# Sample's small products on 128 rows, head norms in place, and two weights split ahead, in a one-core encoder step

## The chip, the cores and the metric

The kernel runs on one core of one Trainium2 chip, as one launch. The metric is the time of an execution on the device in microseconds. A core has a matrix engine (PE), a vector engine (DVE), an activation engine (ACT), a general engine (POOL) and SP, which issues transfers; POOL issues transfers too. Each engine works through its own queue in order, and waits on semaphores for the others.

## The reference

One layer of a hybrid encoder, for a prompt of 512 tokens and a sample of 64 tokens, both 1024 wide, in fp32:

```python
x = x + mixer(rmsnorm(x))        # gated delta rule (4 heads of 128) and gated linear attention, merged by gates
x = x + cross_attn(rmsnorm(x))   # 4 heads of 256 into 256 memory tokens
x = x + conv_ffn(rmsnorm(x))     # 1024 -> 2*2816, causal conv of width 3, silu gate, -> 1024
y = rmsnorm(x)
```

In the delta rule each chunk needs the inverse of a lower triangular matrix:

```python
a_kk = where(strict, einsum('nbhcd,nbhsd->nbhcs', kb, kc) * decay, 0.0)
wu = triangular_solve(eye + a_kk, rhs, lower=True, unit_diagonal=True)
```

The outputs are both y, and the states of both branches, of the convolutions, and the memory's keys and values. What the text calls Prompt and Sample are the 512 and the 64 tokens.

## The kernel before

Activations stand transposed, features on the 128 partitions and all 576 tokens along the free axis, in 128-feature tiles x. A product with a 1024-wide weight runs over eight such tiles. To keep fp32 accuracy each operand is split into a rounded part and a rest (xh and xl, the weight's two tiles w), and three products are summed: high by high, high by rest, rest by high.

A weight comes twice from HBM. SP loads it to a raw tile (wr). ACT writes its negative to the rest's tile and its rounded copy to the high tile, and POOL issues a DMA that adds the weight once more to the rest's tile (`split_summed`), which leaves the rounding error. So a weight's high part is ready when ACT is through, its rest only when that DMA has landed. Raw tiles are four, weight tiles six until the middle of the kernel. `emit_weight(i)` writes these steps for the i-th weight; `fetch(i)` does so for as many as there are tiles for; `weight(...)` takes a weight and gives the tiles of older ones back.

At the start three weights (the first head's q, k, v) are split part by part while x comes in (`wpart`). PE multiplies all three together (`first3`), 144 matmuls. Then come the copies of its results out of PSUM (`conv_raw`, tiles u, two on DVE and the third on ACT), the squares for the norm (`sq_act`, sums in acc), a small product with w0 on 32 columns, the norm's sums (`ssq`), and the fourth weight (`za`, head 0), which is the second that the wording of the change counts. The norm's factors (rt, by a power on POOL) are spread over the partitions with a diagonal matrix (dg) and ones on PE, give rbc, and scale the gates' rows (ba).

All other work is written as chains (generators): `c_gdn(h)` for a delta-rule head, h = 0 to 3 for Prompt and 4 for all heads of Sample; `c_gla(p)` for a pair of linear-attention heads; `c_att(hd)` for an attention head. A planner (`Driver`) runs them beside the main sequence of projections. It keeps a clock for PE and lists of busy times for DVE, ACT and POOL, with costs per instruction and due times of tiles, and it writes each engine's instructions in order of planned start, up to 6 us (BACK) ahead of PE's place. The order on each engine is fixed thereby when the kernel is built. When a buffer comes free is part of the plan, so the number of slots (NS, of SLOT columns each) has a say in the order. X stands for DVE or POOL, whichever the plan finds earlier.

Line 292 of the profile is the recording helper's one call, and stands for all planned instructions; so groups are told apart by the tiles' names. sm is any PSUM bank.

In `c_gdn` the inverse is built in five levels (LEVELS 2, 4, 8, 16, 32). A level transposes the odd blocks of the inverse so far (xo, in xi) on PE, multiplies the odd keys (no, from N) with its even blocks, masks that (bd), multiplies with the transposed copy (yc), and subtracts. For Prompt n = 128 rows, two of each product a level; for Sample n = 64, one of each. An fp32 matmul that is no transpose is recorded as two passes. For Prompt a lower block is then made with N and T2 (tile T): rows 0 to 63 cleared by POOL, rows 64 to 127 copied by DVE.

`head_norm` and `head_norms` take the squares of the outputs ot (or os), scale into a new slot (on) and transpose that. In `c_att` probabilities e stand in three tiles, two for Prompt and one with 64 rows for Sample, and are transposed on PE.

Of the kernel before, what the change touches and what calls it, by code (L numbers as in the profile page):

```python
# [17 lines left out]
P = 128  # L18
D = 1024
TP = 512  # L20
# [2 lines left out]
KT = D // P  # L23
EPS = 1e-6
NJ = 22
SLOT = 584
HT = T // 2
NS = 57
RAWB = 4
NBANK = 8  # L30
SPARE = 2
# [481 lines left out]
def tile_trunk(ctx, tc, xT, memT, wt, wd, vec, cst, w0, wgate, st_gdn, st_conv, st_gla, st_ffn, ckT, cv,  # L513
# [344 lines left out]

    def sum_tile(w=T):
        acc = slot("acc")  # L860
        G.memset(acc[:, w:w + 8], 0.0)
        return acc

    def ssq(accs, t, n, ps):
# [8 lines left out]
    def c_rstat(key, accs, n, sample, delay, out=None, at=TP):  # L873

        yield [accs[0][0]]
        rt = cp.tile([P, 8], F32, name=nm("rt"))
        ps = sm()
        for t in range(n):
            ssq(accs, t, 128, ps)
        rin = tiny(8, "rin")  # L880
        k = n
        if sample:
            k += 1
            ssq(accs, n, 72, ps)
            G.memset(rin, 1.0)
            V.tensor_scalar(rin[0:64, n:n + 1], ps[0:64, n:n + 1], 1.0 / D, EPS, op0=ALU.mult, op1=ALU.add)
        V.tensor_scalar(rin[:, 0:n], ps[:, 0:n], 1.0 / D, EPS, op0=ALU.mult, op1=ALU.add)
        G.tensor_tensor(rt[:, 0:k], rin[:, 0:k], mhalf[:, 0:k], op=ALU.pow)
        yield
        rh, rl = cp.tile([P, 8], F32R, name=nm("rh")), cp.tile([P, 8], F32, name=nm("rl"))  # L890
        V.tensor_copy(rh[:, 0:k], rt[:, 0:k])
        V.tensor_tensor(rl[:, 0:k], rt[:, 0:k], f(rh[:, 0:k]), op=ALU.subtract)
        dgs = []
        for r_ in (f(rh), rl):
            dg = slot("dg", F32R)
            V.tensor_tensor(r4(dg[:, :n * 128]), ident.unsqueeze(1).broadcast_to([P, n, 128]),
                            r_[:, 0:n].unsqueeze(2).broadcast_to([P, n, 128]), op=ALU.mult)
            if sample:
                V.tensor_scalar(dg[:, TP:TP + TS], ident[:, 0:64], r_[:, n:n + 1], None, op0=ALU.mult)
            dgs.append(dg)  # L900
        yield
        out = out or slot("rbc")
        ps = sm()
        for i, dg in enumerate(dgs):
            PE.matmul(ps[:, :n * 128], ones_r, dg[:, :n * 128], start=i == 0, stop=i == 1)
        A.copy(out[:, :n * 128], ps[:, :n * 128])
        if sample:
            ps2 = sm()
            for i, dg in enumerate(dgs):
# [173 lines left out]
    def head_norms(*tiles):  # L1083
# [10 lines left out]
        yield  # L1094
        ons = []
        for (o3, n, k), ss in zip(tiles, sums):
            on3 = r4(slot("on")[0:n, 0:128 * k])
            V.tensor_tensor(on3, o3, ss[0:n, 0:k].unsqueeze(2).broadcast_to([n, k, 128]), op=ALU.mult)
            ons.append(on3)
        yield  # L1100
# [8 lines left out]
    def head_norm(o3, n, k, box, rq=None):  # L1109
# [13 lines left out]
        on = slot("on")  # L1123
        on3 = r4(on[0:n, 0:128 * k])
# [10 lines left out]
    def c_gdn(h):  # L1135
# [91 lines left out]
        V.tensor_tensor(col(SX), col(SX), pd[0:n, 0:4], op=ALU.mult)  # L1227

        xi = slot("xi")
        for i in range(4):  # L1230
            V.scalar_tensor_tensor(xi[0:n, n * i:n * i + n], pk[0:n, n * i:n * i + n], rr[0:n, 4 * SX + i:4 * SX + i + 1],
                                   negm1[0:n, 0:n], op0=ALU.mult, op1=ALU.mult)
# [8 lines left out]
            return ap.rearrange("p (a s b) -> p a s b", s=2, b=b)[:, :, 0, :]  # L1241

        def odd_keys(li):
            no = small(f"no{me}", 2, 256)
            A.copy(no[0:n, 0:w].rearrange("p (a b) -> p a b", b=LEVELS[li]), odd(N_.rearrange("p a b -> p (a b)"), LEVELS[li]))
            return no

        no = odd_keys(0)
        xo = small(f"xo{me}", 1, 256)
# [10 lines left out]
        for li, b in enumerate(LEVELS):  # L1260
            pt = sm()
            for c in range(w // 128):
                PE.transpose(pt[:, n * c:n * c + n], xo[0:n, 128 * c:128 * c + 128], ident[0:n, 0:n])
            yc = small(f"yc{me}", 1, 256)
            if n == 128:
                A.copy(yc[:, 0:256], pt[:, 0:256])
# [1 line left out]
                A.copy(r4(yc[:, 0:128], 64), pt[:, 0:64].unsqueeze(1).broadcast_to([P, 2, 64]))  # L1268
            p1 = sm()
            for c in range(w // 128):  # L1270
                PE.matmul(p1[:, 128 * c:128 * c + 128], no[0:n, 128 * c:128 * c + 128], even(xi[0:n, 256 * c:256 * c + 256], b), start=True, stop=True)
            bd = small(f"bd{me}", 1, 256)
            lm = const(M_LEV + 128 * li)
            V.tensor_tensor(r4(bd[:, 0:w]), r4(p1[:, 0:w]), lm.unsqueeze(1).broadcast_to([P, w // 128, 128]), op=ALU.mult)
            if b < LEVELS[-1]:
                no = odd_keys(li + 1)
                xo = small(f"xo{me}", 1, 256)
# [21 lines left out]
        A.copy(yt[0:n, 0:W], px[0:n, 0:W])  # L1299
        if n == 128:  # L1300
            pt2 = sm()
            tt = slot("T2")
            G.memset(tt[0:64, 0:256], 0.0)
            for i in range(4):
                PE.matmul(pt2[64:128, 64 * i:64 * i + 64], N_[:, i, 64:128], xi3[:, i, 0:64], start=True, stop=True)
            V.tensor_copy(tt[64:128, 0:256], pt2[64:128, 0:256])
            yield
            pu = sm()
# [39 lines left out]
        for i in range(4 if h < 4 else 0):  # L1348
            ci = 4 * i + h
            if S is not None:  # L1350
                pc = sm()
                PE.matmul(pc[0:n, 0:128], ks_[i], S, start=True, stop=True)
                R = small("R", 4)[0:n, :]
# [41 lines left out]
    def c_gla(p):  # L1395
# [35 lines left out]
            yield WAIT  # L1431
        ks = N["kb", p]
        kx, kg = slot("kx"), slot("kg")
        G.memset(kg[:, T:T + 8], 0.0)
# [7 lines left out]
        PE.transpose(pt2[0:72, 0:128], kg[:, TP:T + 8], ident)  # L1442
# [103 lines left out]
    def c_att(hd):  # L1546
# [4 lines left out]
        for g in range(3):  # L1551
# [14 lines left out]
            V.tensor_reduce(sc[0:n, 0:cnt_], r4(pss[0:n, 0:256 * cnt_], 256), axis=AX.X, op=ALU.max)  # L1566
            V.tensor_scalar(sc[0:n, 0:cnt_], sc[0:n, 0:cnt_], -1.0 / 16, None, op0=ALU.mult)
            e = slot("e")
            for i in range(cnt_):
                A.activation(e[0:n, 256 * i:256 * i + 256], pss[0:n, 256 * i:256 * i + 256], AF.Exp,  # L1570
                             bias=sc[0:n, i:i + 1], scale=1.0 / 16, accum_out=sc[0:n, 2 + i:3 + i])
# [21 lines left out]
        A.copy(pst, pS[:, 0:128])  # L1593
        yield
        while not drv.ready(("v", hd)):
            yield WAIT
# [114 lines left out]
    def main():  # L1711
# [895 lines left out]
```

## Time and profile before

| | |
|---|---|
| median of 3 runs | 1081.94 us (1079.63, 1081.94, 1083.07) |
| profiled execution | 1078.61 us, span from first to last instruction 1076.8 us |
| mean granted clock of PE | 0.997 |
| busy: PE, DVE, ACT, POOL | 99%, 70%, 66%, 34% |
| moved | 171 MB, a mean of 159 GB/s |

A row of the time line reads: start and length in us, engine, line, operation, tile written <- tiles read, rows and columns of the array (PE), shape, count of merged instructions, and in brackets the idle time ahead and what ended it. PE's records overlap, since matmuls are pipelined: what one costs is seen from start to start.

### The profile page before, as it was taken

How to read it: one execution, taken by the hardware profiler on the slowest of the kernel's cores; microseconds unless marked ns; L12 is line 12 of the kernel's file. 1: busy time of each engine (PE TensorE's matmuls, PEld its weight loads, DVE VectorE, ACT ScalarE, POOL GpSimd, SP SyncE). 2: the span in 40 equal slices, each digit the busy share in tenths (PEclk: the TensorE clock that was granted, in tenths of full speed). 3: DMA queues.
4: the chain of work that ended last, by engine and by line, in shares of the span. 5: the costliest groups of instructions: out<-in, count | busy, mean ns of one | idle time of the engine just before them, and what ended most of it. 6: DMA issues, size and time to landing. Idle time of an engine off the chain costs nothing.

```text
span 1076.8 us, 21403 instructions
## 1 busy us (share of the span) xinstructions
PE 1065.5 (99%) x8162; PEld 1048.5 (97%) x8162; DVE 751.3 (70%) x1472; ACT 706.9 (66%) x1410; POOL 363.4 (34%) x584
## 2 busy tenths in 40 slices
PE   9899999999999999999999999999999999999997
PEld 8899999999999999999999999999999999999997
DVE  6666854767665776878647766778877776678665
ACT  6665546564667577456666678768776775777645
POOL 0334225344434333114211235344343333332324
PEclk9999999999999999999999999999999999999999
DMA  7656354454437979679674368758887798778844
GB/s 270 158 124 154 61 135 110 95 123 106 99 58 167 252 171 199 237 208 238 172 186 138 63 161 198 180 115 166 185 192 173 153 217 189 181 159 190 185 87 109
DMA packets 68182, 171.33 MB, mean 159 GB/s; under 512 B 7920, under 2 KB 14576, under 8 KB 68080
## 3 DMA queue, kind: packets, MB, share of 16 engines
q0 software_dynamic: 30672, 71.19, 38.4%
q1 hardware_dynamic: 36976, 98.26, 27.6%
q8 instruction: 64, 1.05, 0.4%
q10 hardware_dynamic: 432, 0.53, 0.1%
q14 instruction: 38, 0.31, 0.1%
HBM read 157.50 MB, written 5.37 MB: 151 GB/s over the span
## 4 chain that ended last, share of the span: by engine, by line
PE 95%; DMA 2%; ACT 1%; DVE 1%; issue 0%; POOL 0%; ACTq 0%; DVEq 0%; POOLq 0%
PE sm L292 95%; DMA w<-wt 2%; ACT w L292 1%; PE warm L292 0%; DVE on L292 0%; ACT jk L292 0%; DVE ws L292 0%; DVE x L292 0%; DVE gt L292 0%; DVE acl L292 0%; DVE yo L292 0%; ACT ao L292 0%; DVE S L292 0%; ACT ach L292 0%; ACT xh L292 0%
## 5 line engine op out<-in xcount | busy, mean ns | idle before, releaser
L292 PE MATMUL sm<-xh,w 128*128 128x290 f32 (+3 forms) x2304 | 448.6, 301 | 3.7 <-DMA w<-wt 3.2
L292 PEld LDWEIGHTS sm<-xh,w 128*128 128x128 f32 x2304 | 358.8, 190 | 6.2 <-DMA w<-wt 3.7
L292 PE MATMUL sm<-xl,w 128*128 128x290 f32 (+3 forms) x1152 | 270.6, 296 | 0.0
L292 POOL DMA_DIRECT2D w<-wt x152 | 135.1, 898 | 348.3 <-ACT w L292 296.5
L292 PE MATMUL sm<-ach,w 128*128 128x288 f32 (+2 forms) x1212 | 231.4, 296 | 0.2 <-DVE x L292 0.2
L292 PEld LDWEIGHTS sm<-xl,w 128*128 128x128 f32 x1152 | 200.7, 189 | 0.2 <-DVE xl L292 0.2
L292 PEld LDWEIGHTS sm<-ach,w 128*128 128x128 f32 x1212 | 189.8, 188 | 1.2 <-ACT w L292 0.6
L292 ACT CAST w<-wr 128x512 fp32r<-128x512 f32 (+5 forms) x209 | 159.2, 764 | 15.2 <-PE sm L292 9.6
L292 ACT ACTIVATE w<-wr 128x512 fp32r<-128x512 f32 (+5 forms) x186 | 142.2, 765 | 27.0 <-PE sm L292 25.8
L292 PE MATMUL sm<-acl,w 128*128 128x256 f32 (+2 forms) x606 | 146.6, 295 | 0.2 <-DVE acl L292 0.2
L292 ACT CAST w<-ws 128x512 fp32r<-128x512 f32 (+1 forms) x136 | 80.2, 597 | 49.9 <-DVE ws L292 26.9
L292 PEld LDWEIGHTS sm<-acl,w 128*128 128x128 f32 x606 | 107.3, 188 | 0.5 <-DVE acl L292 0.5
L292 DVE TENSOR_TENSOR w<-ws,w 128x512 fp32r<-128x512 f32 (+1 forms) x107 | 72.8, 689 | 22.6 <-ACT w L292 20.8
L292 DVE SCALAR_TENSOR_TENSOR fc<-fu,vec,fc 128x578 f32<-128x578 f32 x88 | 70.5, 816 | 3.3 <-ACT fc L292 3.3
L292 PE MATMUL sm<-sh,w 128*128 128x290 f32 x288 | 61.5, 298 | 0.0
L292 DVE TENSOR_TENSOR x<-x,sm 128x320 f32<-128x320 f32 (+3 forms) x98 | 40.1, 438 | 22.8 <-PE sm L292 22.5
L292 POOL DMA_DIRECT2D w<-wd x34 | 29.8, 886 | 75.1 <-ACT w L292 67.6
L292 ACT ACTIVATE fc<-fu,vec 128x578 f32<-128x578 f32 x44 | 38.1, 871 | 15.1 <-POOL fu L292 14.8
L292 PEld LDWEIGHTS sm<-sh,w 128*128 128x128 f32 x288 | 47.6, 189 | 0.0
L292 PE MATMUL sm<-oh,w 128*128 128x256 f32 (+1 forms) x256 | 44.8, 295 | 0.0
L292 DVE TENSOR_TENSOR ws<-ws,wr 128x512 f32<-128x512 f32 (+1 forms) x66 | 43.8, 663 | 1.0
L292 PE MATMUL sm<-sl,w 128*128 128x290 f32 x144 | 39.7, 297 | 0.0
(391 smaller groups left out, 1947.9 us busy)
## 6 DMA issues: line engine op xcount, KB each, us to landing
wr<-wt SPq DMA_DIRECT2D x129, 512.0 KB, 5.6
w<-wt POOLq DMA_DIRECT2D x51, 512.0 KB, 6.7
w<-wt POOLq DMA_DIRECT2D x101, 256.0 KB, 6.1
w<-ws POOLq DMA_DIRECT2D x27, 256.0 KB, 5.1
x<-xT SPq DMA_DIRECT2D x16, 288.0 KB, 5.9
wr<-wt SPq DMA_DIRECT2D x14, 256.0 KB, 5.2
wr<-wd SPq DMA_DIRECT2D x8, 448.0 KB, 5.0
w<-wd POOLq DMA_DIRECT2D x8, 448.0 KB, 6.7
```

The lines of the kernel that those rows point to most:

```text
L292: fn(*args, **kw)
```

## The change

- Sample's inverse: xi takes a whole slot on 128 rows, of which POOL clears rows 64 to 127; xo and no are columns 256 to 511 of the same slot. The transposes and the first product of each level use all 128 rows. In attention rows 64 to 127 of Sample's e are cleared, and its two transposes use 128 rows. The rows added hold zeros.
- Head norms write the scaled outputs over ot and os.
- T2 lies in N, so that its clear comes after the four products that read N.
- NS goes from 57 to 59, SLOT from 584 to 582, so that the clears and products of the padding have 70 columns instead of 72; R has two buffers instead of four.
- At the start, the four late squares, the giving back of the first three weights, and the emission of weights 3 and 4 are written ahead of the copies of the first product.

```diff
-SLOT = 584
+SLOT = 582
-NS = 57
+NS = 59
...
-            on3 = r4(slot("on")[0:n, 0:128 * k])
+            on3 = o3
             V.tensor_tensor(on3, o3, ss[0:n, 0:k].unsqueeze(2).broadcast_to([n, k, 128]), op=ALU.mult)
...
         xi = slot("xi")
+        rows = P if n == 64 else n
+        if n == 64:
+            G.memset(xi[64:128, 0:512], 0.0)
...
-            no = small(f"no{me}", 2, 256)
+            no = small(f"no{me}", 2, 256) if n == 128 else xi[:, 384:512]
...
-                PE.transpose(pt[:, n * c:n * c + n], xo[0:n, 128 * c:128 * c + 128], ident[0:n, 0:n])
+                PE.transpose(pt[:, 128 * c:128 * c + 128], xo[0:rows, 128 * c:128 * c + 128], ident)
...
-                PE.matmul(p1[:, 128 * c:128 * c + 128], no[0:n, 128 * c:128 * c + 128], even(xi[0:n, 256 * c:256 * c + 256], b), start=True, stop=True)
+                PE.matmul(p1[:, 128 * c:128 * c + 128], no[0:rows, 128 * c:128 * c + 128], even(xi[0:rows, 256 * c:256 * c + 256], b), start=True, stop=True)
...
-            tt = slot("T2")
-            G.memset(tt[0:64, 0:256], 0.0)
             for i in range(4):
                 PE.matmul(pt2[64:128, 64 * i:64 * i + 64], N_[:, i, 64:128], xi3[:, i, 0:64], start=True, stop=True)
+            tt = N_[:, 0:2, :].rearrange("p a b -> p (a b)")
+            G.memset(tt[0:64, 0:256], 0.0)
...
+            if g == 2:
+                G.memset(e[64:128, 0:256], 0.0)
...
-            PE.transpose(pS[:, 64 * mt_:64 * mt_ + 64], probs[2][0:64, 128 * mt_:128 * mt_ + 128], ident[0:64, 0:64])
+            PE.transpose(pS[:, 128 * mt_:128 * mt_ + 128], probs[2][:, 128 * mt_:128 * mt_ + 128], ident)
...
+        for k in range(4, KT):
+            sq_act(k)
+        for i in range(3):
+            drop(*wready.pop(i))
+        emit_weight(3)
+        emit_weight(4)
         raw_u = [conv_raw(ps, copy) for ps, copy in zip(first3, (V.tensor_copy, V.tensor_copy, A.copy))]
         fetch(3)
-        for k in range(4, KT):
-            sq_act(k)
```

How the order moves, at three places. On ACT, at the start, behind the squares (sq); wr is a raw weight, w a split one, u a copy of the first product. Before:

```order
L292 ACTIVATE sq_317<-x_89 128x576
L292 COPY u_313<-sm_135 128x256
L292 COPY u_313<-sm_136 128x256
L292 COPY u_313<-sm_136 128x64
L292 ACTIVATE w_357<-wr_355 128x1024
L292 CAST w_356<-wr_355 128x1024
L292 ACTIVATE w_360<-wr_358 128x1024
L292 CAST w_359<-wr_358 128x1024
```

and now:

```order
L292 ACTIVATE sq_314<-x_89 128x576
L292 ACTIVATE w_317<-wr_315 128x1024
L292 CAST w_316<-wr_315 128x1024
L292 ACTIVATE w_320<-wr_318 128x1024
L292 CAST w_319<-wr_318 128x1024
L292 COPY u_323<-sm_135 128x256
L292 COPY u_323<-sm_136 128x256
L292 COPY u_323<-sm_136 128x64
```

The four instructions of both splits moved ahead of the three copies.

On POOL, at the same place; the DMA rows are the adding transfers, rt the norm's power. Before:

```order
L292 MEMSET rin_353 128x8
L292 DMA w_357<-wt 128x1024
L292 ISA
L292 TENSOR_TENSOR rt_341<-rin_353,mhalf 128x5
L292 DMA w_360<-wt 128x1024
L292 DMA w_363<-wt 128x1024
```

and now:

```order
L292 DMA w_317<-wt 128x1024
L292 MEMSET rin_366 128x8
L292 DMA w_320<-wt 128x1024
L292 MEMSET u_321 128x3
L292 DMA w_326<-wt 128x1024
L292 ISA
L292 TENSOR_TENSOR rt_353<-rin_366,mhalf 128x5
```

Three transfers, not one, now stand ahead of the power.

On PE, at the second delta-rule head, where T2 (now in N) is used; R and vg belong to the first head's chain, xh are projections. Before:

```order
L292 MATMUL sm_2067<-xi_1589,N_1586 64x64 x4
L292 MATMUL sm_2075<-R_2051,Y_1677 128x128
L292 MATMUL sm_1953<-xh_124,w_1643 128x256
L292 MATMUL sm_1954<-xh_124,w_1643 128x320
L292 MATMUL sm_1953<-xh_126,w_1643 128x256
L292 MATMUL sm_1954<-xh_126,w_1643 128x320
L292 MATMUL sm_2087<-Y_2066,T_2068 64x64 x4
```

and now:

```order
L292 MATMUL sm_2066<-xi_1589,N_1586 64x64 x4
L292 MATMUL sm_2072<-R_2050,Y_1677 128x128
L292 MATMUL sm_1952<-xh_124,w_1643 128x256
L292 MATMUL sm_1953<-xh_124,w_1643 128x320
L292 MATMUL sm_1952<-xh_126,w_1643 128x256
L292 MATMUL sm_1953<-xh_126,w_1643 128x320
L292 MATMUL sm_2089<-xh_112,w_1819 128x256
L292 MATMUL sm_2090<-xh_112,w_1819 128x320
L292 MATMUL sm_2089<-xl_113,w_1819 128x256
L292 MATMUL sm_2090<-xl_113,w_1819 128x320
L292 MATMUL sm_2096<-Y_2065,N_1586 64x64 x4
```

Four matmuls of the next projection moved ahead of the use.

More of the change, by code (lines that the diff above doesn't have):

```diff
@@ L860, in sum_tile @@
         acc = slot("acc")
-        G.memset(acc[:, w:w + 8], 0.0)
+        G.memset(acc[:, w:w + 6], 0.0)
         return acc
@@ L883, in c_rstat @@
             k += 1
-            ssq(accs, n, 72, ps)
+            ssq(accs, n, 70, ps)
             G.memset(rin, 1.0)
@@ L1122, in head_norm @@
         yield
-        on = slot("on")
-        on3 = r4(on[0:n, 0:128 * k])
+        on3 = o3
         V.tensor_tensor(on3, o3, ss[0:n, 0:k].unsqueeze(2).broadcast_to([n, k, 128]), op=ALU.mult)
@@ L1248, in c_gdn @@
         no = odd_keys(0)
-        xo = small(f"xo{me}", 1, 256)
+        xo = small(f"xo{me}", 1, 256) if n == 128 else xi[:, 256:384]
         A.copy(xo[0:n, 0:w].rearrange("p (a b) -> p a b", b=2), odd(xi[0:n, 0:W], 2))
@@ L1276, in c_gdn @@
                 no = odd_keys(li + 1)
-                xo = small(f"xo{me}", 1, 256)
+                xo = small(f"xo{me}", 1, 256) if n == 128 else xi[:, 256:384]
                 xo_ = xo[0:n, 0:w].rearrange("p (a s b) -> p a s b", s=2, b=b)
@@ L1352, in c_gdn @@
                 PE.matmul(pc[0:n, 0:128], ks_[i], S, start=True, stop=True)
-                R = small("R", 4)[0:n, :]
+                R = small("R", 2)[0:n, :]
                 V.scalar_tensor_tensor(R, pc[0:n, 0:128], sg[0:n, NE, ci:ci + 1], vb[:, i, :], op0=ALU.mult, op1=ALU.add)
@@ L1433, in c_gla @@
         kx, kg = slot("kx"), slot("kg")
-        G.memset(kg[:, T:T + 8], 0.0)
+        G.memset(kg[:, T:T + 6], 0.0)
         V.tensor_tensor(kg[:, 0:T], ks[:, 0:T], e3[:, 0:T], op=ALU.mult)
@@ L1441, in c_gla @@
         pt2 = sm()
-        PE.transpose(pt2[0:72, 0:128], kg[:, TP:T + 8], ident)
+        PE.transpose(pt2[0:70, 0:128], kg[:, TP:T + 6], ident)
         for a in range(2):
@@ L1590, in c_att @@
         for mt_ in range(2):
-            PE.transpose(pS[:, 64 * mt_:64 * mt_ + 64], probs[2][0:64, 128 * mt_:128 * mt_ + 128], ident[0:64, 0:64])
+            PE.transpose(pS[:, 128 * mt_:128 * mt_ + 128], probs[2][:, 128 * mt_:128 * mt_ + 128], ident)
         pst = small("pst", 2)
-        A.copy(pst, pS[:, 0:128])
+        A.copy(r4(pst, 64), r4(pS[:, 0:256])[:, :, 0:64])
         yield
```

## The prediction

> **What bounds the kernel now.** I read the page first, then PE's waits, the chain in order of time, and the time lines of the stages that the change touches.
>
> ```profile
> PE 1065.5 (99%) x8162; PEld 1048.5 (97%) x8162; DVE 751.3 (70%) x1472; ACT 706.9 (66%) x1410; POOL 363.4 (34%) x584
> PE sm L292 <- DMA w<-wt: 3.2, 2, 2.8
> PE sm L292 <- ACT gt L292: 0.4, 1, 0.4
> PE sm L292 <- DVE T L292: 0.2, 1, 0.2
> ```
>
> PE is busy for 99% of the span. It waits for one thing of any size, a weight DMA. So a microsecond saved on DVE, ACT or POOL is worth nothing, and one saved on PE, as a wait or as a slot of the array, counts in full unless a later wait takes it back.
>
> **The start: the second weight.** PE's time line (start, length) round that wait, ACT's and POOL's beside it, two pieces of the chain, and two windows (the number after the engines is the granted clock, then the DMA share):
>
> ```profile
> 32.37 0.42 PE L292 MATMUL sm<-xh,w 128*128 128x256 f32 x2
> 32.63 0.43 PE L292 MATMUL sm<-xl,w 128*128 128x256 f32 x2
> 35.90 0.80 PE L292 MATMUL sm<-xh,w 128*128 128x256 f32 x4 [2.84 <-DMA w<-wt]
> 36.54 0.77 PE L292 MATMUL sm<-dg,onesr 128*128 128x512 f32 x4
> 37.15 3.18 PE L292 MATMUL sm<-xh,w 128*128 128x256 f32 x12
> 40.12 1.41 PE L292 MATMUL sm<-cst,ba 128*128 128x8 f32 x10
> 15.62 4.12 ACT L292 ACTIVATE sq<-x 128x576 f32<-128x576 f32 x7
> 25.43 0.77 ACT L292 COPY u<-sm 128x256 f32<-128x256 f32 x3 [5.69 <-PE sm L292]
> 26.07 1.08 ACT L292 ACTIVATE w<-wr 128x1024 fp32r<-128x1024 f32 x1
> 27.46 1.05 POOL L292 DMA_DIRECT2D w<-wt  x1 [24.57 <-ACT w L292]
> 29.20 1.19 POOL L292 TENSOR_TENSOR rt<-rin,mhalf 128x5 f32<-128x5 f32 x1 [0.69 <-DVE rin L292]
> 6.06 19.34 PE sm L292 x143
> 27.46 8.39 DMA w<-wt
> 22.00:25.40 3.40, 3.40 (x27) 3.30 (x25) 1.54 (x6) 0.00 (x0) 0.00 (x0) 1.00 0.02 6
> 37.14:40.56 3.42, 3.42 (x18) 3.42 (x17) 2.30 (x6) 1.17 (x4) 1.10 (x4) 0.51 1.08 279
> ```
>
> ACT stands idle for 5.69 us behind the copies of the first product, which need PE's end at 25.43. Only after them comes the split of the second weight (26.07), then the adding DMA, issued at 27.46 and landed 8.39 later, at 35.85. PE had run out at 32.63 + 0.26 = 32.89 (rows stand 0.26 apart), so it lost 35.90 - 32.89 = 3.0 us.
>
> The change puts both splits before the copies. ACT is free at 15.62 + 4.12 = 19.74. The raw weight has landed by 22.00 at the latest, since the DMA share is 0.02 from there on. So the split starts between 19.7 and 22.0, POOL issues 1.4 later as now (27.46 - 26.07), at 21.1 to 23.4, and with 8.39 to land the sum is there at 29.5 to 31.8. That is 1.1 to 3.4 us before PE asks. The tiles it writes are those of the first two weights, which PE last reads at one and two thirds of the product that runs from 6.06 to 25.40, so at 12.5 and 19.0: free in time. SP's next raw loads wait for these splits and move ahead with them, into a stretch with a DMA share of 0.02. The wait goes: **3.0 us**. Bounds 3.0, and 0 if the earlier issue finds something that the trace can't show; both ends of the computed landing give 3.0, and I take it.
>
> The second loss stands right behind. In the window 37.14:40.56 the granted clock was 0.51. Twelve matmuls took 40.12 - 37.15 = 2.97; at the spacing before the gap they take 6 x 0.26 = 1.56, with 0.09 for the first after the fp32 ones (0.22 against 0.13 in the rows further down) 1.65. So 1.3 us more goes if PE is not left idle. Bounds 0 and 1.3, and I take **1.3**, since the slow window begins right behind that gap. [...]
>
> What is late next? PE reaches the normalizer's diagonal (dg) and the gates' operand (ba) 3.0 us earlier, and ba with 1.3 us less ahead of it.
>
> ```profile
> 32.08 1.12 DVE L292 TENSOR_SCALAR dg<-keep,rl 128x64 fp32r<-128x64 f32 x1
> 37.82 0.82 DVE L292 TENSOR_TENSOR ba<-sm,rbc 128x256 f32<-128x256 f32 x2 [4.62 <-ACT rbc L292]
> ```
>
> dg is complete at 33.20. PE comes to dg at 36.54 - 3.0 = 33.5, and first to its wide half. ba is complete 1.49 after 37.15; PE needs it 1.65 after. Both just fit, by 0.3 and 0.16 us. POOL's power (rt, 29.20) now stands behind three DMA issues instead of one. The third follows the third split, which moves up to about 26.1 on ACT, so it ends near 27.46 + 1.05 = 28.5, before rin frees rt at 29.2. Cost 0; if that cover goes, rt, dg and PE slip together.
>
> **The products on 64 rows.** One level of Sample's inverse in PE's time line, 64-row rows first, then 128-row fp32 ones, and the same for attention with the count of forms:
>
> ```profile
> 313.62 0.29 PE L292 MATMUL sm<-xl,w 128*128 128x288 f32 x1
> 313.85 0.27 PE L292 MATMUL sm<-keep,xo 64*128 64x64 f32 x1
> 313.95 0.44 PE L292 MATMUL sm<-xi,no 64*128 64x128 f32 x2
> 314.32 0.40 PE L292 MATMUL sm<-xh,w 128*128 128x288 f32 x1
> 314.56 0.29 PE L292 MATMUL sm<-xl,w 128*128 128x288 f32 x1
> 314.69 0.39 PE L292 MATMUL sm<-R,Y 128*128 128x128 f32 x2
> 314.83 0.38 PE L292 MATMUL sm<-xh,w 128*128 128x288 f32 x1
> 315.05 0.29 PE L292 MATMUL sm<-xl,w 128*128 128x288 f32 x1
> 328.40 0.60 PE L292 MATMUL sm<-keep,on 128*128 128x128 f32 x4
> 328.75 0.77 PE L292 MATMUL sm<-xh,w 128*128 128x288 f32 x4
> 556.50 1.30 PE L292 MATMUL sm<-keep,e 128*128 128x128 f32 x10
> 557.74 0.53 PE L292 MATMUL sm<-xh,w 128*128 128x256 f32 x2
> L292 PE MATMUL sm<-keep,xo x45: 270/272/328, 87.7 to 329.5; 128*128 128x128 f32 x40, 64*128 64x64 f32 x5
> L292 PE MATMUL sm<-keep,e x40: 222/272/275, 556.5 to 618.7; 128*128 128x128 f32 x32, 64*128 64x64 f32 x8
> ```
>
> Starts tell what a matmul costs the array. Two fp32 passes on 128 rows take 314.83 - 314.69 = 0.14, four take 0.35, so one more is 0.105. The first ordinary one behind takes 0.22 (314.83 to 315.05) instead of 0.13. A level's xl, transpose, two passes and xh take 314.56 - 313.62 = 0.94 on 64 rows; on 128 rows 0.13 + (0.14 + 0.105) + 0.22 = 0.60. Saved 0.34, five levels (xo x5): **1.7 us**. Attention's ten transposes, two of them on 64 rows, take 557.74 - 556.50 = 1.24; ten on 128 rows 0.35 + 6 x 0.105 = 0.98. Saved 0.26, four heads (x8 of two): **1.0 us**. Bounds: nothing, if the cost came from elsewhere than the rows, and 2.8, if the slower ordinary matmul behind (0.24) gains its 0.02 too.
>
> [...]
>
> **What is added.** Nine POOL clears: five new ones (Sample's tile, and attention's four heads), and Prompt's four of T2, which ran early and now, in N, wait for the products that read N.
>
> ```profile
> 158.12 0.65 POOL L292 MEMSET T<- 64x256 f32 x1
> 159.48 1.56 POOL L292 MEMSET aqb<- 128x512 f32 x3
> 168.35 0.43 DVE L292 COPY T<-sm 64x256 f32<-64x256 f32 x1 [1.64 <-PE sm L292]
> 169.19 0.68 PE L292 MATMUL sm<-Y,T 128*64 128x64 f32 x8
> 170.65 0.88 POOL L292 DMA_DIRECT2D w<-wt  x1 [9.60 <-ACT w L292]
> ```
>
> At the second head POOL stands idle from 161.0 to 170.6, while DVE copies the other half from 168.35 to 168.78. A clear let go by the same products runs beside that copy (0.65 us at most), and PE, which used T at 169.19, now has four more matmuls (4 x 0.13) ahead of that. Cost 0, by that cover. If it is gone at all nine, 9 x 0.65 = 5.9 us is the upper bound; the lower is 0. Norms in place, the two buffers more, and 70 columns for 72 remove no instruction of weight. They only move the planner's order: PE's order is the old one up to 169 us and again from about 635 us. Between, the waits for gt and T in the first fence (0.6) may go or come again: bounds -0.6 and +2, taken 0.
>
> **The sum**: 3.0 + 1.3 + 1.7 + 1.0 = 7.0 us. The profiled execution took 1078.61 (span 1076.8), 3.3 below the median 1081.94; its like would be 1071.6, and the median 1081.94 - 7.0 = **1074.9**. About 0.3% (3.2 us) is what a measurement tells from no change.
>
> **Rivals.**
> *The clock term is this run's alone* (windows fall otherwise, or a short wait at dg or ba takes its place): for it, 0.16 and 0.3 us of spare are thin; against, 0.51 is plain. 1076.2, still faster. 0.11. [...]
> *The 64-row forms cost no more than the 128-row ones*: against it, every level's rows. 1077.6. 0.02. [...]
> *New waits in the reordered stretch, or behind the clears, take 4 to 7 us*: for it, PE waits for only 0.6 there now, so that another order can hardly take away and can add, and nine clears hang on an in-order queue; against, DVE and ACT have 30% to spare. 1079 to 1082: no change. 0.13.
> *Slower: a clear stands behind a POOL issue that waits for ACT.* The row at 170.65 shows the queue held 9.60 us by one. If PE comes to the use 1.4 after the products let go (169.19 + 0.52 - 168.35), it stands 8.2, and a slow clock window adds 1.3: two such places give 1074.9 + 19 = 1093.9. One gives 1084.4, which is still within 0.3%. It decides from a total wait of 10.2 us on. Against: the order has such an issue right ahead at few of them. 0.05.
> *The waits for gt and T vanish too*: 1074.3, or lower by what other order brings. 0.05.
> My forecast: 0.64. So faster 0.82, same 0.13, slower 0.05. The range runs from 1071.0 (the profiled execution, 1078.61, as base, and the waits for gt and T gone) to 1080.3 (the slowest of the three runs, 1083.07, as base, the clock term and half of the clears' bound lost).
>
> **What would show it.** After: PE's wait for DMA w<-wt at the start gone, POOL's first issue near 21 to 23 us, clock 1.00 between 34 and 42; no 64-row keep,xo, keep,e; levels at 0.60 us. Wrong if PE waits for POOL (N, e, xi, rt), if dg or ba become its releaser, or if the middle shows new waits for ACT or DVE of over 3 us.

## The result, and the profile after

The changed kernel takes 1069.79 us (median of 5 runs, 1069.41 to 1070.45). The kernel before took 1081.94 in 5 runs beside it (1079.16 to 1083.63). The ratio is 0.9896, interval 0.9877 to 0.9916: 12.15 us faster. The forecast of 1074.9 had the direction, but 1069.8 lies below its range, which began at 1071.0. Run beside the kernel before once more (experiment 5), the change gave 0.9911 (0.9898 to 0.9925), 9.44 us.

The profiled executions took 1078.61 and 1069.41 us, 9.20 apart. Span and busy times on the page of the changed kernel:

```profile
span 1067.6 us, 21403 instructions
PE 1059.3 (99%) x8162; PEld 1044.6 (98%) x8162; DVE 749.7 (70%) x1480; ACT 705.0 (66%) x1410; POOL 356.5 (33%) x581
```

Two of the largest waits of PE for products that are left (us in total, times, longest):

```profile
PE sm L292 <- ACT gt L292: 0.4, 1, 0.4
PE sm L292 <- DMA w<-wt: 0.3, 1, 0.3
```

The wait for weights was 3.2 in two places and is 0.3 in one: at the start PE no longer waits for one, and the 0.3 stands between 619 and 719 us, where the kernel before had 0.4. PE is still busy for 99%, with 6 us less to do: half-clock time and slow 64-row products are counted as busy (in the first trace of before 3.41 of 3.41 us from 37.21 on, at a clock of 0.50, and 0.94 of 0.94 us in the level from 313.62 to 314.56), so the share could not show them.

At the start, the time lines of PE, ACT, POOL and DVE in the changed kernel:

```profile
32.31 0.43 PE L292 MATMUL sm<-xl,w 128*128 128x256 f32 x2
32.58 0.69 PE L292 MATMUL sm<-xh,w 128*128 128x256 f32 x4
33.11 0.77 PE L292 MATMUL sm<-dg,onesr 128*128 128x512 f32 x4
33.71 1.84 PE L292 MATMUL sm<-xh,w 128*128 128x256 f32 x12
35.40 1.17 PE L292 MATMUL sm<-cst,ba 128*128 128x8 f32 x10
16.10 4.12 ACT L292 ACTIVATE sq<-x 128x576 f32<-128x576 f32 x7
20.16 1.06 ACT L292 ACTIVATE w<-wr 128x1024 fp32r<-128x1024 f32 x1
25.10 0.77 ACT L292 COPY u<-sm 128x256 f32<-128x256 f32 x3 [1.05 <-PE sm L292]
21.53 1.05 POOL L292 DMA_DIRECT2D w<-wt  x1 [18.68 <-ACT w L292]
27.11 0.86 POOL L292 DMA_DIRECT2D w<-wt  x1 [2.71 <-ACT w L292]
28.88 1.20 POOL L292 TENSOR_TENSOR rt<-rin,mhalf 128x5 f32<-128x5 f32 x1 [0.90 <-DVE rin L292]
34.39 0.82 DVE L292 TENSOR_TENSOR ba<-sm,rbc 128x256 f32<-128x256 f32 x2 [2.37 <-ACT rbc L292]
```

And its window where the granted clock had been 0.51 (the clock is the third number from the end):

```profile
37.14:40.56 3.42, 3.42 (x22) 2.70 (x21) 3.00 (x9) 2.59 (x6) 0.93 (x1) 1.00 0.01 4
```

The rest part's first product (32.58) now follows the high part's last (32.31) without a gap. The split starts at 20.16, right behind the squares, and the adding DMA is issued at 21.53. Twelve matmuls that took 2.97 from start to start take 1.69 (33.71 to 35.40), at a clock of 1.00.

One level of Sample's inverse, and one head's ten transposes, in PE's time line of the changed kernel:

```profile
321.89 0.30 PE L292 MATMUL sm<-acl,w 128*128 128x288 f32 x1
322.03 0.27 PE L292 MATMUL sm<-keep,xi 128*128 128x128 f32 x1
322.13 0.39 PE L292 MATMUL sm<-xi 128*128 128x128 f32 x2
322.28 0.38 PE L292 MATMUL sm<-ach,w 128*128 128x288 f32 x1
322.49 0.29 PE L292 MATMUL sm<-acl,w 128*128 128x288 f32 x1
550.83 1.25 PE L292 MATMUL sm<-keep,e 128*128 128x128 f32 x10
551.84 1.42 PE L292 MATMUL sm<-xh,w 128*128 128x256 f32 x9
```

From product to product the level takes 322.49 - 321.89 = 0.60 (it was 0.94), the ten transposes 551.84 - 550.83 = 1.01 (it was 1.24).

**Where the 9.1 us of the traces lie.** Both kernels issue 8162 matmuls, so each can be set against the one of the same number. By how much the changed kernel is ahead, at times of the kernel before:

| at | ahead, us | gained since the row above |
|---|---|---|
| 13 us | 0.32 | 0.32, warm-up |
| 60 us | 4.97 | 4.65, the start |
| 304 us | 5.61 | 0.64, reordered stretch |
| 332 us | 7.42 | 1.81, Sample's inverse |
| 440 us | 6.49 | -0.93 |
| 556 us | 6.73 | 0.24 |
| 619 us | 7.85 | 1.12, four attention heads |
| end | 9.09 | 1.24 |

The two kernels issue their matmuls in different orders round 304 us, so that row is rough. What stands in it and in the next is sure only in sum, 2.45: from product to product the five levels of Sample's inverse take 2.94 instead of 4.67, and the waits for gt (0.4, between 320 and 330 us) and T (0.2, between 260 and 290) are gone. The warm-up is no gain: two more executions of the unchanged kernel differ from the first there by 0.26 and 0.39. The loss before 440 us is for the most part one new wait, seen in the time lines of ACT and PE of the changed kernel:

```profile
403.59 1.06 ACT L292 ACTIVATE w<-wr 128x1024 fp32r<-128x1024 f32 x1 [0.63 <-ACT gt L292]
404.56 1.03 ACT L292 CAST w<-wr 128x1024 fp32r<-128x1024 f32 x1
405.49 1.25 ACT L292 ACTIVATE gt<-gt 128x576 f32<-128x576 f32 x2
406.00 0.70 PE L292 MATMUL sm<-xh,w 128*128 128x288 f32 x4
407.08 0.40 PE L292 MATMUL sm<-ach,w 128*128 128x288 f32 x1 [0.38 <-ACT gt L292]
```

The plan puts a 2 us weight split ahead of the gates (gt), and PE comes to a stop for their bank: four matmuls take 1.08 from start to start instead of 0.53.

### The profile page after: what moved, and what is told of

The parts are those of the page before. It is cut to its first block, busy times and chain, and to the rows that moved or that the text cites. A ratio compares the mean times of both kernels' runs of the same rounds, so it can differ in the third digit from the quotient of the medians.

```text
span 1067.6 us, 21403 instructions
## 1 busy us (share of the span) xinstructions
PE 1059.3 (99%) x8162; PEld 1044.6 (98%) x8162; DVE 749.7 (70%) x1480; ACT 705.0 (66%) x1410; POOL 356.5 (33%) x581
## 4 chain that ended last, share of the span: by engine, by line
PE 96%; DMA 1%; ACT 1%; issue 0%; DVE 0%; SPq 0%; ACTq 0%
PE sm L292 96%; DMA w<-wt 1%; ACT w L292 1%; DMA wr<-wt 0%; ACT gt L292 0%; DVE w L292 0%; DVE x L292 0%; DVE acl L292 0%; DVE yo L292 0%; ACT ao L292 0%; ACT ach L292 0%; ACT xh L292 0%; DVE xl L292 0%; SPq L292 0%; DVE ws L292 0%
```

## The experiments

The kernel before ran beside each series: medians 1078.61 (23 runs, with experiments 1 to 4), 1078.82 (15, with 5 to 8), 1078.33 (9, with 9 to 12) and 1078.76 (23, with 13 and 14). "Below" and "above" are against the one of its series; the interval follows.

**1. The start alone** (edit to the kernel before)

```diff
+        for k in range(4, KT):
+            sq_act(k)
+        for i in range(3):
+            drop(*wready.pop(i))
+        emit_weight(3)
+        emit_weight(4)
         raw_u = [conv_raw(ps, copy) for ps, copy in zip(first3, (V.tensor_copy, V.tensor_copy, A.copy))]
         fetch(3)
-        for k in range(4, KT):
-            sq_act(k)
```

> The kernel before with one part of the change: late squares, giving back of the first three weights, and weights 3 and 4 ahead of the copies of the first product. Theory A (the forecast's two terms, wait 3.0 and clock 1.3, and nothing that varies from run to run): 4.3 us below the kernel before, about 1077.6 of 1081.9, and the runs spread as those of before do (some 4 us). Theory B (the wait for the second weight costs the median run more than the profiled one, because the clock's window falls differently in each run): 7 to 8 us below, about 1074.5, with the runs within some 1.5 us of each other. Theory C (the missing microseconds come from the slots' stride or number): 4.3 below, as A.

1073.44 (1072.94 to 1073.95): 5.2 below, 4.2 to 7.5. The size lies nearer to A's 4.3 than to B's 7 to 8, the spread of 1.0 speaks for B: the kernel before spread over 6.4 in this series. In the trace it is 4.9 ahead from 42 us on and 4.85 at 619.

**2. All but the start** (edit to the changed kernel)

```diff
-        for k in range(4, KT):
-            sq_act(k)
-        for i in range(3):
-            drop(*wready.pop(i))
-        emit_weight(3)
-        emit_weight(4)
         raw_u = [conv_raw(ps, copy) for ps, copy in zip(first3, (V.tensor_copy, V.tensor_copy, A.copy))]
         fetch(3)
+        for k in range(4, KT):
+            sq_act(k)
```

> The changed kernel without the part at the start (weights 3 and 4 split behind the copies, as before); rows, head norms, slots and buffers as changed. Theory A: 4.3 us above the changed kernel, about 1074.1, that is 7.9 below the kernel before. Theory B: about 1077, 7 to 8 above the changed kernel, and a spread of some 4 us, as before has. Theory C: about 1074.1 with a small spread.

1074.60 (1074.12 to 1075.78): 4.0 below, 2.8 to 6.3. The wait is back (PE idle 3.0 us for the DMA), with a stretch of 3.41 us at half clock. Against the changed kernel of experiment 5 that is some 5.2, though in another series. A has the size; the spread of 1.7 lies between A's and B's.

**3. The 128 rows alone** (the core of the edit to the kernel before)

```diff
+        rows = P if n == 64 else n
+        if n == 64:
+            G.memset(xi[64:128, 0:512], 0.0)
...
-                PE.transpose(pt[:, n * c:n * c + n], xo[0:n, 128 * c:128 * c + 128], ident[0:n, 0:n])
+                PE.transpose(pt[:, 128 * c:128 * c + 128], xo[0:rows, 128 * c:128 * c + 128], ident)
...
+            if g == 2:
+                G.memset(e[64:128, 0:256], 0.0)
...
-            PE.transpose(pS[:, 64 * mt_:64 * mt_ + 64], probs[2][0:64, 128 * mt_:128 * mt_ + 128], ident[0:64, 0:64])
+            PE.transpose(pS[:, 128 * mt_:128 * mt_ + 128], probs[2][:, 128 * mt_:128 * mt_ + 128], ident)
```

> The kernel before with the products of Sample's inverse and the transposes of Sample's e on 128 rows alone. Theories A, B and C: five levels at 0.34 and four heads at 0.25 to 0.26, so 2.7 us below the kernel before, about 1079.2; in the trace the transpose and first product of a level take 0.60 from start to start instead of 0.94. A rival: the planner's order moves, and 1 to 2 us are lost or gained elsewhere.

1078.17: 0.4 below, 2.0 below to 0.2 above. The 2.7 is not seen, but the levels take 0.60 all the same. The rival holds. The time lines of PE, ACT and POOL of this kernel, first at a wait for gt (1.0, where the kernel before waits 0.4 and the changed one no longer waits), then where the four heads' outputs are projected:

```profile
323.83 0.40 PE L292 MATMUL sm<-ach,w 128*128 128x288 f32 x1 [1.00 <-ACT gt L292]
359.80 0.53 PE L292 MATMUL sm<-oh,w 128*128 128x256 f32 x2 [0.35 <-ACT oh L292]
360.60 0.53 PE L292 MATMUL sm<-ol,w 128*128 128x256 f32 x2 [0.26 <-DVE ol L292]
362.54 0.54 PE L292 MATMUL sm<-ol,w 128*128 128x256 f32 x2 [0.48 <-POOL ol L292]
359.08 2.39 ACT L292 CAST oh<-og 128x576 fp32r<-128x576 f32 x4 [2.21 <-DVE og L292]
360.98 1.50 POOL L292 TENSOR_TENSOR ol<-og,oh 128x576 fp32r<-128x576 f32 x1 [3.44 <-ACT oh L292]
```

The same casts in ACT's time line of the changed kernel:

```profile
349.79 1.25 ACT L292 CAST oh<-og 128x576 fp32r<-128x576 f32 x2 [2.23 <-DVE og L292]
351.98 1.25 ACT L292 CAST oh<-og 128x576 fp32r<-128x576 f32 x2
```

Here the new order lets Sample's chain end late. Its outputs (oh) are cast at 359.08, just when PE asks for them; in the kernel before it was from 354.6 on, in the changed one, whose PE is 7.5 ahead there, from 349.79 on without a wait behind it. PE's lead over the kernel before falls from 1.4 at 358 us to -0.8 at 364: the plan gives 2.2 back at one place. At gt it had lost 0.6 more, so that the lead grows by 1.15 over the five levels (304 to 358 us) and not by 1.7.

**4. The slots' part alone** (the core of the edit to the kernel before)

```diff
-SLOT = 584
+SLOT = 582
-NS = 57
+NS = 59
...
-            on3 = r4(slot("on")[0:n, 0:128 * k])
+            on3 = o3
...
-            tt = slot("T2")
...
+            tt = N_[:, 0:2, :].rearrange("p a b -> p (a b)")
...
-                R = small("R", 4)[0:n, :]
+                R = small("R", 2)[0:n, :]
```

> The kernel before with head norms in place, T2 in N, two R buffers, 59 slots of 582 columns and 70 columns of padding alone: neither the part at the start nor the 128 rows. Theory A: within 1 us of the kernel before, about 1081.9, as the forecast put this part at 0 (bounds -0.6 and +2). Theory B: the same. Theory C (stride or number of slots makes each matmul behind the middle some 0.3% shorter, 1.2 us in the trace of the changed kernel): 1 to 3 us below, 1079 to 1081.

1077.94 (1075.70 to 1081.76): 0.7 below, 1.8 below to 1.0 above, as A and B said. The mean clocks of its 12 runs went from 0.992 to 0.999; the trace has a stretch of 6.83 us at half clock, twice as long as that of the first trace of before. So the median hides something: from 60 us to the end this kernel gains 2.1 on the kernel before in the traces, 0.9 of it behind 619 us, and its waits for gt and T are gone, as in the changed kernel. At the start it loses 1.5 to the longer stretch.

**5. The changed kernel once more**

> The changed kernel once more, beside the kernel before on the same chip as the runs of this call. The kernel before has given medians of 1081.9 and 1078.6 in two series. Theory A (parts add up: start 5.2, rows 0.4, slots 0.7, as measured apart): 6.3 us below the kernel before. Theory D (rows and slots are worth more together than apart, as the two together without the start gave 4.0): 4.0 + 5.2 = 9.2 below, some 1069.5 where the kernel before has 1078.6. Both: a spread of about 1 us, since PE no longer runs dry at the start and the granted clock stays at 0.999 in every run.

1069.38 (1069.12 to 1069.70): 9.4 below, 8.1 to 11.0. D: by the medians the parts are worth 5.2 + 0.4 + 0.7 = 6.3 apart and 9.4 together, though the 0.7 is low for the clocks of its runs (experiment 4). The spread of 0.6 is as expected.

**6. PE kept busy in the wait** (added to the kernel before, ahead of the rest part of the second weight's product; NFILL is 13)

```diff
+        for _ in range(NFILL):
+            PE.matmul(pd, ones_r, ones_r.unsqueeze(1).broadcast_to([P, 4, 128]), start=True, stop=True)
```

> The kernel before with 13 products of ones (128x512, into a spare bank) put on PE between the high and the rest part of the second weight's product, just where PE waits some 3 us; they change no result. The wait for the weight stays, but PE is not idle in it. Theory E (what PE loses beyond the wait, and the spread of the kernel before, is the clock halved after the idle stretch): no stretch at a granted clock of 0.5 near 37 us, 0.999 in all runs, a spread of about 1 us, and a median 1.5 to 2.5 us below that of the kernel before; it ends near those runs of the kernel before that had 0.999 (1076.6). Rival: the half clock comes from the kernel's load or a fixed place in time and not from the idleness: clock and median as before, or 0.5 us above for the added products.

1077.15 (1076.32 to 1078.18): 1.7 below, 0.8 to 2.7. PE's time line (all planned instructions stand at line 293 here):

```profile
32.66 3.13 PE L293 MATMUL sm<-onesr 128*128 128x512 f32 x13
36.02 0.80 PE L293 MATMUL sm<-xh,w 128*128 128x256 f32 x4 [0.23 <-DMA w<-wt]
37.26 1.83 PE L293 MATMUL sm<-xh,w 128*128 128x256 f32 x12
38.92 1.16 PE L293 MATMUL sm<-cst,ba 128*128 128x8 f32 x10
```

The weight lands as late as before (36.02), so nothing of the wait is saved. But the twelve matmuls take 1.66 from start to start (37.26 to 38.92) instead of 2.97, no stretch is at half clock, and all mean clocks lie between 0.998 and 1.000. So here the half clock follows from the idleness, and it is worth 1.7 us in the median beside the wait. The spread fell to 1.9, not to 1.

**7. Slots of 584 columns in the changed kernel**

```diff
-SLOT = 582
+SLOT = 584
```

The edit leaves the padding at 70 columns.

> The changed kernel with slots of 584 columns (and 72 of padding) instead of 582; still 59 slots. Theory C (the stride of the slots makes matmuls 0.3% shorter behind the middle): 1 to 2 us above the changed kernel, and the lag behind it grows steadily from 650 us to the end. Rival (the stride is nothing, the number of slots sets the plan): within 0.7 us of the changed kernel, whatever the order of a few instructions makes.

1070.16: 0.8 above experiment 5, with overlapping runs (1069.64 to 1070.58 against 1069.12 to 1069.70). What the changed kernel gains behind 619 us is here too (1.12), so theory C falls.

**8. Start and rows, without the slots' part** (edit to the changed kernel; head norms, T2 and four R buffers as before, too)

```diff
-SLOT = 582
+SLOT = 584
-NS = 59
+NS = 57
...
```

> The kernel before with the part at the start and the 128 rows, but without the slots' part (head norms in place, T2 in N, two R buffers, 59 slots of 582). Theory A (parts add up): 5.2 + 0.4 = 5.6 below the kernel before, and 0.7 above the changed kernel. Theory D (the rows' 2.7 are there, but the plan with 57 slots gives 2.3 of them back where PE waits for the outputs ol near 360 us, behind a DMA issue on POOL and late work on ACT): the same 5.6 below before, but some 3.6 above the changed kernel, with the waits of PE for ol and oh in the trace at the same place as with the rows alone. Rival: the earlier start moves ACT's and POOL's work so that these waits go: 7.9 below before.

1072.01 (1071.99 to 1073.65): 6.8 below, 5.2 to 7.9, and 2.6 above the changed kernel. A and D had 5.6 below; 2.6 above the changed kernel is nearer to D's 3.6 than to A's 0.7, and the place is D's: PE waits for oh and ol again, from 355 to 358 us, with 0.35, 0.26 and 0.49 ahead of its products, as in experiment 3. So the rival with 7.9 below, by which these waits go, falls, though 6.8 is as near to it. In the profiled execution, the run of 1073.65, the clock fell right behind these waits:

```profile
358.26:361.68 3.42, 3.42 (x16) 3.42 (x16) 3.03 (x6) 2.19 (x5) 1.43 (x2) 0.50 0.53 77
```

The others, with 0.998 or 0.999, took 1072.0 to 1072.6.

**9 and 10. Start and rows with a piece of the slots' part each** (edits to experiment 8, the first for 9, the second for 10)

```diff
-            on3 = r4(slot("on")[0:n, 0:128 * k])
+            on3 = o3
```

```diff
-SLOT = 584
+SLOT = 582
-NS = 57
+NS = 59
...
-                R = small("R", 4)[0:n, :]
+                R = small("R", 2)[0:n, :]
```

> The kernel before with the part at the start, the 128 rows, and of the slots' part only the head norms in place (57 slots of 584, T2 in its own slot, four R buffers). Reference values beside the kernel before: 6.8 below without any slots' part, 9.4 below with all of it. Theory F (the slot that head_norm takes for its scaled output is what Sample's chain waits for): 9 below, no wait of PE for ol and oh near 355 us. Theory G (the number of slots moves the whole plan, and where Sample's chain falls in it is chance): 6 to 8 below, the casts oh of Sample's heads stay where they were or move either way.

> The kernel before with the part at the start, the 128 rows, and of the slots' part the 59 slots of 582 columns, 70 columns of padding and two R buffers (head norms in a slot of their own, T2 in its own slot). Theory F: 6 to 7 below the kernel before, with the wait for ol and oh as with the rows alone. Theory G or the number of slots by itself: 8.5 to 9.4 below, the casts oh of Sample's heads some 5 us earlier than with the rows and the start alone.

Both 1072.35: 6.0 below (5.1 to 8.0, and 4.6 to 7.3). Both traces have the waits for oh and ol again, with Sample's casts from 354.05 and 354.30 on (349.79 in the changed kernel). So F falls by experiment 9, and the number of slots by itself, which was to give 8.5 to 9.4 below, by experiment 10: neither piece takes the waits away alone. In experiments 2, 5 and 7, with all pieces or all but the stride, they are gone. Which pair of them does it was not tried, nor T2 in N without more slots.

**11 and 12. Two more traces of the kernel before**

> The kernel before, unchanged, for a second trace. Theory H (the 1.1 to 1.4 us by which the changed kernels gain steadily behind 620 us, at 0.3% per matmul, differ from execution to execution): the trace goes away from the first trace of before by some 0.3 to 1 us between 620 us and the end. Rival (it belongs to the program): the two agree there within 0.2 us. At the start: a wait of 2.5 to 3.4 us and zero, one or more stretches of 3.41 us at half clock, which decide its time, at 0.9 us for each 0.001 of the mean clock.

> The kernel before, unchanged, for a third trace; expected as for the second. If the mean clock of the two differs, their difference up to 60 us should be the difference of their stretches at half clock, halved.

1079.50 and 1077.98. The stretch at half clock as a window of the second trace:

```profile
34.88:41.71 6.83, 5.89 (x24) 5.70 (x24) 2.29 (x6) 1.33 (x5) 1.10 (x4) 0.50 1.04 264
```

and of the third:

```profile
36.06:39.48 3.42, 3.42 (x15) 3.23 (x14) 1.65 (x5) 0.70 (x2) 0.17 (x1) 0.50 1.07 277
```

In the second the clock fell while PE was still waiting, and stayed down for 6.83; in the third for 3.42, as in the first. The twelve matmuls, wholly at half clock in the second, take 3.03 there (38.08 to 41.11), against 1.66 in experiment 6. Taken as half of the time in which PE works, an estimate from the clock of 0.50, the loss is 5.89 / 2 = 2.9 against 1.7, so 1.2 should lie between the two, and their PE starts differ by 1.34 over the stretch (from 0.13 ahead of the wait to 1.47 at matmul 280), 0.2 of which is the later landing (PE goes on at 35.82 and 35.46). From there to 619 us the three traces run side by side within 0.03 us. Behind it they differ by 0.1 to 0.2, where the changed kernel gains 1.24: the rival holds, that gain belongs to the program. The edited kernels bear this out. Every one with the rows or the slots' part gains 0.9 to 1.4 there, experiment 1 gains 0.4, and experiments 6, 13 and 14 gain 0.1 to 0.2, about as much as the repeats.

**13. Half of the wait filled** (edit to experiment 6)

```diff
-NFILL = 13
+NFILL = 6
```

> As the kernel with 13 added products of ones in the wait for the second weight, but with 6, so that PE is busy for 1.3 of the 3 us and idle for 1.7 to 2.0. Theory E1 (the length of the idle stretch decides whether the clock falls, and 1.7 us is too short for it): no stretch at half clock, 0.999 in all runs, 1.5 to 2 us below the kernel before. [...]

1076.95 (1076.42 to 1078.72): 1.8 below, 0.9 to 2.9. The trace has no half clock behind 1.34 us of idleness ahead of the rest part (35.51). Eight of 11 runs took 1076.4 to 1077.4; three took 1078.0 to 1078.7, with clocks of 0.998, 0.998 and 0.997 (one of the faster had 0.998 too). The median is as E1 said, the three slower runs are not. In the one with 0.997 the clock must have fallen, by an estimate from its mean: even 0.9975 takes 0.0025 x 1077 / 0.5 = 5.4 us at half clock. The half clock at the end of the run, behind the last matmul, which counts in the mean too, lasts only 1.0 to 3.6 us in the traces (2.0 in the first of before, from 1074.86 on, and in that of the changed kernel, from 1065.56 on). For the two with 0.998 it is not settled.

**14. The weight 3 us later** (edit to the kernel before)

```diff
         raw_u = [conv_raw(ps, copy) for ps, copy in zip(first3, (V.tensor_copy, V.tensor_copy, A.copy))]
+        for k in range(5):
+            A.activation(slot("sq")[:, 0:512], raw_u[2][:, 3:515], AF.Square)
         fetch(3)
```

> The kernel before with five further squares (128x512, about 0.6 us each, read by nothing) on ACT between the copies of the first product and the split of the second weight, so that its sum lands some 3 us later and PE waits some 6 us; the planner also moves a few instructions behind that. Theory E (the half clock follows from the idle stretch and lasts longer after a longer one): wait 6 us, mean clocks of 0.992 to 0.996, and 4 to 6 us above the kernel before, 3 of them the wait. A first series with a median of 1081.9 for the kernel before would then be one in which the weight landed later or the clock stayed low for longer. Rival (one stretch of 3.41 us whatever the wait's length): 3 us above the kernel before, with the same clocks and spread as that.

1080.54 (1078.80 to 1083.40): 1.8 above, 0.5 to 3.2, with clocks from 0.994 to 0.998. PE's time line where it goes on:

```profile
38.69 1.18 PE L292 MATMUL sm<-xh,w 128*128 128x256 f32 x4 [3.04 <-DMA w<-wt]
```

and the window of the half clock:

```profile
38.88:45.71 6.83, 6.83 (x21) 4.71 (x21) 2.41 (x8) 0.44 (x2) 0.00 (x0) 0.50 0.85 221
```

But the planner put the normalizer's product (dg) into the gap and added a wait of 2.0 us for the high part, so that PE waited in two pieces and not 6 us in one. The experiment does not tell its theories apart. 1.8 lies below both.

**All runs of the kernel before together.** 70 runs in the four series, by mean granted clock:

| clock | runs | mean us | from, to |
|---|---|---|---|
| 0.999 | 5 | 1076.84 | 1076.51, 1077.32 |
| 0.998 | 23 | 1078.40 | 1077.08, 1079.26 |
| 0.997 | 22 | 1078.63 | 1077.81, 1079.52 |
| 0.996 | 16 | 1079.90 | 1079.29, 1080.33 |
| 0.995 | 1 | 1081.74 | |
| 0.993 | 3 | 1083.28 | 1082.93, 1083.55 |

A line through them falls by 0.96 us for each 0.001 (correlation -0.92), which is about what a mean of 0.001 less of 1077 us is worth. So the clock explains most of the spread of 7 us. The traces of before with one stretch of 3.41 us have 0.997, the one with 6.83 has 0.996. A mean of 0.999 leaves no room for a stretch (0.0015 x 1077 / 0.5 = 3.2 us at half clock at most); one of 0.998 can be with a stretch or without, since the time behind the last matmul counts in it too.

## Why the forecast was too small

**The wait, 3.0: right.** The lead grows by 4.65 from 13 to 60 us; the half clock, 0.51 in the window of 3.42 us, takes about half of that, 1.7 by estimate, and what is left is 3.0. The steps came as computed: split at 20.16 (19.7 to 22.0), issue at 21.53 (21.1 to 23.4), rt at 28.88 behind the third issue, which ends at 27.97 (28.5 was forecast). The diagonal is there in time, and so is ba, at 35.21 for a use at 35.40, of which the forecast had said that it just fits.

**The clock, 1.3: right in kind, too small in size.** In the two profiled executions it is that 1.7, since the stretch goes on behind the twelve, to 40.62, and the products there ran slowly too. In the median of the runs it is 1.7 by experiment 6 (0.8 to 2.7). The rival "the clock term is this run's alone" falls: 42 of 70 runs of the kernel before have a mean clock of 0.997 or less, so by the estimate of experiment 13 they must hold half-clock time ahead of the end; five have 0.999, which leaves no room for a stretch. The three traces of before have one of 3.41, 6.83 and 3.41 us, which begins at 37.21, 34.88 and 36.06.

**The 128 rows, 1.7 and 1.0: right.** 0.60 for the level shown and 0.57 to 0.60 for the others, 1.73 saved by the five; 1.01 per head for 0.98. The lead grows by 1.12 over the four heads. But experiment 3 shows that they were no 2.7 us by themselves.

**The clears and the new order, 0: near zero in the sum, by luck.** The changed kernel gains 0.64 and 0.24 and loses 0.93 outside the places of the change, -0.05 together. The waits for gt and T, which the forecast had as its bound of -0.6, are gone, and a new one for gt near 407 us (0.55 from start to start) takes most of that back. PE waits for none of the clears, so the rival by which one stands behind an issue on POOL did not come. The same rows under 57 slots lose 2.2 where ol is late and 0.6 at gt, the price of the rival "new waits in the reordered stretch" by half. The forecast gave head norms, T2 and slots no worth. Alone they show none in the medians (experiment 4: 0.7, with an interval about 0), though 2.1 in the trace; together with the rows they are worth 2.6 (experiments 5 and 8). The order showed only which instructions move, and what a move costs depends on the whole plan.

**Behind 619 us, nothing forecast, 1.24 gained.** PE's order is the old one there. From matmul 4850 to 8160 the three traces of before take 444.21, 444.10 and 444.04, the changed kernel 443.00 and, in experiment 5, 443.10: 0.3 ns for each. That is an average over matmuls of which some are faster and some slower. The slots' stride is not the cause (experiment 7), and the rows or the slots' part alone bring most of it (experiments 3 and 4). The cause is open.

**The step that failed: the sum was made in one execution and taken off the median of three runs, and what lies behind 619 us was put at nothing.** Worked from the profiled execution, 1078.61 - 7.0 = 1071.6; the changed kernel's took 1069.41, so the sum of the terms is 2.2 short: 0.3 of warm-up, 0.35 of the start, 1.24 of the tail, 0.2 of the stretches with the rows, and 0.1 behind the last matmul. The low end of the range, 1071.0, already had the profiled execution as its base. What it missed is therefore this part, and above all the tail: the forecast held the order to be the old one there and counted nothing, and the runs show 1.24.

The other 2.9 are the distance of the median from the profiled execution, 3.3 before and 0.4 after. The forecast took this distance as a constant of the kernel. It is none: in the 70 later runs of the kernel before the median is 1078.62, which is the profiled execution's time. The first series (1079.2 to 1083.6) stood 3 us above them, while the changed kernel's runs beside it stood no higher than later (1069.79 and 1069.38). The wait does spread the runs: with it, the length of the half-clock time differs from run to run (3.41, 6.83 and 3.41 us in the three traces), and without it the runs of the changed kernel lie within 1.0 and 0.6 us. More half-clock time in the first series would explain its height, since three of its five runs took 1081.9 or more, as only three of the 70 later ones did, those at 0.993. But its clocks are not on record, so the cause of this part stays open.

## What to carry to other kernels

When PE bounds the kernel and runs dry for some microseconds, count the wait (3.0 us here), the half-clock time behind it (1.7 in the median, experiment 6), and the spread of the runs that it causes (6.4 in one series, 1.0 where the wait was gone, experiment 1). Under such a spread a median of three runs is a poor base: it was 1081.94 here, and 1078.62 over 70 runs. Price an edit in the plan that it will run in. By the medians the same rows were worth 0.4 us in one plan and 3.3 in another (experiment 3; experiment 2 less experiment 4), by the traces from 60 us on 1.2 and 2.2, and neither edit alone would have shown it.

## What was not expected of the hardware

The granted clock fell to 0.50 after PE had been idle for about 3 us (2.84, 3.02 and 2.79 in the rows of the three traces of before, 3.04 in experiment 14), for 3.41 us in the first and third trace of before and for 6.83 in the second and in experiment 14. By their means of 0.993, three of the 70 runs of the kernel before had more: 0.007 x 1083 / 0.5 = 15 us at half clock by estimate, the time behind the last matmul (1.0 to 3.6 in the traces) among them. The fall came inside the wait in the second trace (34.88, while PE goes on at 35.82), and behind its end by 0.2 us in experiment 14, 0.6 in the third trace and 1.3 in the first. Scattered waits had it behind them once as well: in experiment 8 three within 4 us, which cost 2.2 us from start to start, were followed by 3.42 us at 0.50. In experiment 3 the same waits were not: four matmuls right behind them take 0.61 from start to start (362.92 to 363.53), where two took 0.47 to 0.49 in experiment 8 at 0.50. Nor were they in experiment 10, whose mean of 0.999 leaves no room for such a stretch. What decides it was not shown. Thirteen useless products of 3.1 us made the kernel before 1.7 us faster. And matmuls of one order and shape differed by 0.3 ns each on average between the two programs (443.0 and 443.1 us against 444.0 to 444.2 for 3310 of them), in both traces of the changed kernel against all three of before.
